# Attention in pairs of heads, and a state space branch in pairs of states, in a two-block network on one core

## The chip, the core and the metric

The kernel runs on one core of a Trainium2 chip. The metric is the device time of one execution in microseconds (us). The engines are named as in the profile: TensorE (PE, with its loads of stationary tiles as PEld), VectorE (DVE), ScalarE (ACT), GpSimd (POOL) and SyncE (SP), which here only issues DMAs.

## The reference

One sequence of 256 tokens with 1024 features goes through two blocks. The first adds a mixer with four gated branches (rwkv7, spatial gating, short convolution, state space) and a feed-forward part; the second adds an attention mixer and a feed-forward part that picks experts. What the change touches is the state space branch (16 groups of 16 channels, 64 complex states each)

```python
    bu_re = jnp.einsum('gnc,bsgc->bsgn', bb_re, ug)
    bu_im = jnp.einsum('gnc,bsgc->bsgn', bb_im, ug)
    ...
    _, _, x_re, x_im = lax.associative_scan(_complex_affine_combine, (ar, ai, bu_re, bu_im), axis=1)
    y = (jnp.einsum('gcn,bsgn->bsgc', c_re, x_re) - jnp.einsum('gcn,bsgn->bsgc', c_im, x_im))
```

and the two attentions of the second block, with 8 heads of 64 each. With 256 tokens MoBA's one block is the whole causal sequence, and forgetting attention adds a difference of cumulated log gates to the scores:

```python
    s = (jnp.einsum('bhqd,bhkd->bhqk', qi, k).astype(jnp.float32) * scale
         + cq[..., None] - c[:, :, None, :])
    ...
    s = jnp.where(kpos[None, :] <= qpos[:, None], s, -jnp.inf)
    p = jax.nn.softmax(s, axis=-1).astype(v.dtype)
    return jnp.einsum('bhqk,bhkd->bhqd', p, v)
```

## The kernel before

Activations lie transposed: features on partitions, the 256 tokens along the free axis. `linear` streams weights in units of eight 128x128 tiles (512 KB). For each unit SP loads `raw`, ScalarE rounds it to `whi` (L206), VectorE forms the rest `wlo` (L209), and POOL a part of it where `pool_k` is above 0 (L211). Each buffer exists three times. TensorE runs three matmuls for a tile (`mm3`, L231 to L233), so 24 for a unit, each with 256 tokens. These matmuls are the stream.

The smaller computations are Python generators. `spawn` enters one with a rate, and after each half of a pair of output tiles `linear` calls `tick`, which adds half the rate to its credit and runs a generator for one step per whole credit. So the rate says how many steps of a branch stand between two units of the stream. A scheduler then places the instructions of each engine.

State space: a group of 4 states is folded into 128 partitions, 8 steps `s` in all. `s5_main` (L1040) takes state `s` through: `bu` by two matmuls in a row group of 32 (L1054); products with the tables of cosines and sines (L1057, L1058, VectorE); two sums on POOL give the rotated `z`; two scans (L1064); products back (L1066, L1067); two sums on POOL give `xx` (L1069, L1070); and, two steps later, `project` with two matmuls in a column group of 32 (L1076, L1077). Rate 1.2. Beside it runs the chunked `wkv` (its matmuls L786 to L851, its masked products `kn` on POOL, L814) and the sums of `ada_all` (L426).

Attention: one function for both (L1341 on). A step handles four heads at different stages: scores of head h (L1353, in the row half of 64 that the head's features lie in, with L1355 for the gates in forgetting attention), transposes of head h - 2 (L1360), the softmax of head h - 1 on VectorE and ScalarE (L1367 to L1375), the weighted sum of head h - 3 in a column half of 64 (L1382, L1383). Rates 1.5 and 1.2. `fox_c` prepares the gates: `fw` and `frh` on VectorE (L1336, L1338) and two products into `selh` on POOL (L1337). PSUM tiles of both branches come from a ring of six, "ax".

## Time and profile before

| what | value |
|---|---|
| median of 3 runs | 1589.32 us (1588.9 to 1591.75) |
| the profiled execution, its own time | 1588.85 us |
| its span from the first to the last instruction | 1587.1 us |
| mean granted clock of TensorE | 0.987 of full speed |
| TensorE busy | 1533.5 us, 97% of the span |
| VectorE, ScalarE, POOL busy | 1134.1, 839.8, 358.7 us |
| state space branch beside wkv | from about 115 to 205 us |
| MoBA attention | from about 560 to 625 us |
| forgetting attention | from about 625 to 697 us |

The span is 1.75 us shorter than the time of the same execution. The engines' shares are means over stages with different limits, so each of the three stages is read by itself: its busy times, the waits of TensorE in it, and then single rows. A row of the timeline gives the start, the length, the engine and line, the operation, the tile written and those read, and how many pass records it stands for; neighbours of one kind are one row, and ends of matmuls are modelled, so starts are what is subtracted.

### The profile page before, as it was taken

To read this page: it belongs to the slowest core of one execution; us is meant where nothing else is said; L and a number is where in the kernel's file an instruction comes from. 1 tells how busy PE (TensorE), PEld (TensorE's weight loads), DVE (VectorE), ACT (ScalarE), POOL (GpSimd) and SP (SyncE) were. 2 spreads that over 40 slices of the span, in tenths; PEclk is the share of its full clock that TensorE was granted. 3 is DMA by queue.
4 is the path that set the end of the run, shared out by engine and by line. 5 is a ranking of instruction groups with operands and counts; after the bars stand their busy time and mean duration, and the time that the engine had idled before them with its cause. 6 is when DMAs were issued, how large, how long until landed. Compare 5 with 4: busy or idle time off the path is not lost. (4 is left out here: it accounts for less than half of the span.)

```text
span 1587.1 us, 28930 instructions
## 1 busy us (share of the span) xinstructions
PE 1533.5 (97%) x11462; PEld 1423.3 (90%) x11462; DVE 1134.1 (71%) x1800; ACT 839.8 (53%) x1399; POOL 358.7 (23%) x319
## 2 busy tenths in 40 slices
PE   6998999999999989999999999999999999999997
PEld 5887899999999978899999999999998888888886
DVE  7789886886555675667779967888898555555555
ACT  4563234756543455545445547777776445544443
POOL 7516663345400120004781700000000000000000
PEclk9899899999999999999999999999999999999999
DMA  9445456475556643445555564444544566666663
GB/s 364 153 162 159 158 192 221 152 259 189 187 184 187 189 130 108 130 135 200 173 161 192 167 187 147 146 149 144 150 152 165 174 209 186 191 194 194 193 196 121
DMA packets 75448, 279.67 MB, mean 176 GB/s; under 512 B 8368, under 2 KB 9008, under 8 KB 73648
## 3 DMA queue, kind: packets, MB, share of 16 engines
q1 hardware_dynamic: 75312, 277.82, 54.3%
q8 instruction: 90, 1.47, 0.4%
q14 instruction: 46, 0.38, 0.1%
HBM read 275.69 MB, written 2.10 MB: 175 GB/s over the span
## 5 line engine op out<-in xcount | busy, mean ns | idle before, releaser
L206 ACT ACTIVATE whi<-raw 128x1024 fp32r<-128x1024 f32 x453 | 479.1, 1058 | 551.4 <-PE mm L232 210.8
L209 DVE TENSOR_TENSOR wlo<-raw,whi 128x1024 fp32r<-128x1024 f32 (+2 forms) x413 | 500.2, 1213 | 265.3 <-ACT whi L206 262.2
L231 PE MATMUL mm<-hh,whi 128*128 128x256 f32 x1816 | 525.1, 289 | 3.1 <-ACT gate L581 1.9
L233 PE MATMUL mm<-hh,wlo 128*128 128x256 f32 x1816 | 516.1, 284 | 5.0 <-DVE wlo L209 4.2
L232 PE MATMUL mm<-hl,whi 128*128 128x256 f32 x1816 | 513.0, 282 | 1.1 <-DVE hl L1484 0.7
L231 PEld LDWEIGHTS mm<-hh,whi 128*128 128x128 f32 x1816 | 345.1, 190 | 11.4 <-issue 7.6
L233 PEld LDWEIGHTS mm<-hh,wlo 128*128 128x128 f32 x1816 | 345.8, 190 | 7.4 <-DVE wlo L209 5.0
L232 PEld LDWEIGHTS mm<-hl,whi 128*128 128x128 f32 x1816 | 346.4, 191 | 2.9 <-issue 1.4
L211 POOL TENSOR_TENSOR wlo<-raw,whi 128x256 fp32r<-128x256 f32 (+2 forms) x112 | 186.3, 1668 | 138.7 <-ACT whi L206 85.5
L1518 PE MATMUL ax<-whi,ah 128*128 128x512 f32 x512 | 158.9, 391 | 3.9 <-ACT ah L332 3.9
L1518 PE MATMUL ax<-whi,al 128*128 128x512 f32 x512 | 158.3, 391 | 0.0
L1518 PE MATMUL ax<-wlo,ah 128*128 128x512 f32 x512 | 158.1, 390 | 0.0
L1518 PEld LDWEIGHTS ax<-whi,ah 128*128 128x128 f32 x512 | 96.0, 188 | 23.8 <-ACT ah L332 4.1
L1518 PEld LDWEIGHTS ax<-whi,al 128*128 128x128 f32 x512 | 96.5, 189 | 20.5 <-DVE al L333 0.4
L1518 PEld LDWEIGHTS ax<-wlo,ah 128*128 128x128 f32 x512 | 96.4, 188 | 20.0
L1442 ACT ACTIVATE om<-xres,tg 128x128 f32<-128x128 f32 x256 | 84.9, 392 | 1.0 <-DVE xres L1439 1.0
L233 PE MATMUL ax<-hh,wlo 128*128 128x258 f32 x256 | 72.8, 284 | 1.3 <-DVE wlo L209 1.3
L231 PE MATMUL mm<-fh,whi 128*128 128x256 f32 x256 | 73.0, 285 | 0.0
L233 PE MATMUL mm<-fh,wlo 128*128 128x256 f32 x256 | 72.9, 285 | 0.0
L232 PE MATMUL mm<-fl,whi 128*128 128x256 f32 x256 | 72.9, 285 | 0.0
L231 PE MATMUL ax<-hh,whi 128*128 128x258 f32 x256 | 72.6, 284 | 0.0
L232 PE MATMUL ax<-hl,whi 128*128 128x258 f32 x256 | 72.2, 282 | 0.0
(538 smaller groups left out, 2424.1 us busy)
## 6 DMA issues: line engine op xcount, KB each, us to landing
raw<-in_wts SPq DMA_DIRECT2D x453, 512.0 KB, 3.6
raw<-in_ada SPq DMA_DIRECT2D x24, 512.0 KB, 4.2
araw<-in_ada SPq DMA_DIRECT2D x8, 1024.0 KB, 8.0
w0r<-in_w SPq DMA_DIRECT2D x8, 576.0 KB, 9.0
araw<-in_ada SPq DMA_DIRECT2D x8, 512.0 KB, 4.6
x<-in_x SPq DMA_DIRECT2D x1, 1024.0 KB, 5.1
mb<-in_x SPq DMA_DIRECT2D x2, 512.0 KB, 4.9
selh<-in_att SPq DMA_DIRECT2D x1, 1024.0 KB, 7.2
```

The costliest lines, as they stand in the source:

```text
L206: nc.scalar.activation(hi, raw, AF.Copy)
L209: nc.vector.tensor_tensor(lo[:, :c], raw[:, :c], hi[:, :c].bitcast(FT), op=OP.subtract)
L211: nc.gpsimd.tensor_tensor(lo[:, c:], raw[:, c:], hi[:, c:].bitcast(FT), op=OP.subtract)
L231: mm(ps, wh, xh, start=start, stop=False, **kw)
L232: mm(ps, wh, xl, start=False, stop=False, **kw)
L233: mm(ps, wl, xh, start=False, stop=stop, **kw)
L1442: SC.activation(om[:, j, :], oe[:, j, :], AF.Copy, scale=it["g"][:, t0 + j:t0 + j + 1])
L1518: T.matmul(acc[t][c], a[:, u, z], w[:, c * 512:(c + 1) * 512], start=i + u == 0 and n == 0, stop=i + u == P - 1 and n == 2)
```

## The change

Attention works on pairs of heads. `scores` of a pair interleaves the matmuls of the two row halves, `turn` transposes both heads, `weigh` interleaves the two column halves, and `soft` runs twice in one step. A pair has its own sequence of three steps (scores with the turn of the pair before; softmax; weighted sum), 15 steps instead of 11, and the rates go from 1.5 and 1.2 to 2.05 and 1.65. The tile of scores has four buffers instead of three.

The state space branch works on pairs of states. The bu matmuls of both states stand interleaved in two row groups of 32; the scans write in place; the products after the scan are kept as `v1`, `v2`; POOL's `xx` sums are gone. Instead `project` runs four matmuls for a state, which add the products up in PSUM: with the coefficients of plane 0, of a new plane 2 with the opposite sign, and twice of plane 1. A pair's projection stands directly behind the bu matmuls of the next pair. There are 9 steps instead of 10. In the setup one more VectorE operation fills plane 2.

```diff
@@ -446,7 +446,7 @@
             pa = es.enter_context(tc.tile_pool(name="pa", bufs=1))
             hh, hl = self.hh, self.hl
             self.s5b = pa.tile([P, 2, 2, P], FT, name="s5b")
-            self.s5c = pa.tile([P, 2, 8, 32], FT, name="s5c")
+            self.s5c = pa.tile([P, 3, 8, 32], FT, name="s5c")
             self.tab = pa.tile([P, 2, 8, S], FT, name="s5t")
             self.s5m = pa.tile([P, 8], FT, name="s5m")
             self.masks = pa.tile([P, 3, P], FT, name="masks")
@@ -1008,6 +1008,7 @@
         V.tensor_tensor(c1, craw[:, 0], b(qr), op=OP.mult)
         V.tensor_tensor(c2, craw[:, 1], b(qi), op=OP.mult)
         V.tensor_tensor(self.s5c[:, 0], c1, c2, op=OP.subtract)
+        V.tensor_tensor(self.s5c[:, 2], c2, c1, op=OP.subtract)
         V.tensor_tensor(c1, craw[:, 0], b(qi), op=OP.mult)
         V.tensor_tensor(c2, craw[:, 1], b(qr), op=OP.mult)
         V.scalar_tensor_tensor(self.s5c[:, 1], c1, -1.0, c2, op0=OP.mult, op1=OP.subtract)
@@ -1040,18 +1041,11 @@
     def s5_main(self, psum, pw, u, yo):
         nc, tc = self.nc, self.tc
         V, SC, G, T = nc.vector, nc.scalar, nc.gpsimd, nc.tensor
-        todo, yps = [], {}
-        for s in range(8):
...
+        yps = {}
+
+        def states(s, bu):
             cb = self.tab[:, 0, s:s + 1, :].to_broadcast([P, 2, S])
             sb = self.tab[:, 1, s:s + 1, :].to_broadcast([P, 2, S])
-            bu = psum.tile([P, 2, S], FT, name="ax")
-            for i in range(2):
-                T.matmul(bu[:, i, :], self.s5b[R, h, i, :], u[R, h, :], start=True, stop=True)
             t1, t2 = pw.tile([P, 2, S], FT, name="t1"), pw.tile([P, 2, S], FT, name="t2")
             z = pw.tile([P, 2, S], FT, name="z")
             V.tensor_tensor(t1, bu, cb, op=OP.mult)
@@ -1059,31 +1053,44 @@
             G.tensor_tensor(z[:, 0, :], t1[:, 0, :], t2[:, 1, :], op=OP.add)
             G.tensor_tensor(z[:, 1, :], t1[:, 1, :], t2[:, 0, :], op=OP.subtract)
             m = self.s5m[:, s:s + 1].to_broadcast([P, S])
-            sc = pw.tile([P, 2, S], FT, name="sc")
+            sc = z
             for i in range(2):
                 V.tensor_tensor_scan(sc[:, i, :], m, z[:, i, :], 0.0, op0=OP.mult, op1=OP.add)
-            t1, t2 = pw.tile([P, 2, S], FT, name="t1"), pw.tile([P, 2, S], FT, name="t2")
-            V.tensor_tensor(t1, sc, cb, op=OP.mult)
...
+            v1, v2 = (pw.tile([P, 2, S], FT, name=n, bufs=2) for n in ("v1", "v2"))
+            V.tensor_tensor(v1, sc, cb, op=OP.mult)
+            V.tensor_tensor(v2, sc, sb, op=OP.mult)
+            return v1, v2
+
+        def project(p, vs):
+            h, q = divmod(2 * p, 4)
+            if q == 0:
+                yps[h] = psum.tile([P, S], FT, name="ax")
+            yp = yps[h]
+            for t, (c, j, i) in enumerate(((0, 0, 0), (2, 1, 1), (1, 0, 1), (1, 1, 0))):
+                for a in range(2):
+                    R = slice(32 * (q + a), 32 * (q + a) + 32)
+                    T.matmul(yp[R, :], self.s5c[:, c, 2 * p + a, :], vs[a][j][:, i, :], start=t == 0, stop=t == 3)
+            if q == 2:
+                y = pw.tile([P, S], FT, name="y5", bufs=1)
+                V.scalar_tensor_tensor(y, u[:, h, :], self.v("s5_d", h), yp, op0=OP.mult, op1=OP.add)
+                SC.activation(yo[:, h, :], y, AF.Gelu_apprx_tanh)
+
+        vs = {}
+        for p in range(4):
+            h, q = divmod(2 * p, 4)
             yield
-            project()
+            bus = [psum.tile([P, 2, S], FT, name="ax") for _ in range(2)]
+            for i in range(2):
+                for a in range(2):
+                    R = slice(32 * (q + a), 32 * (q + a) + 32)
+                    T.matmul(bus[a][:, i, :], self.s5b[R, h, i, :], u[R, h, :], start=True, stop=True)
+            if p:
+                project(p - 1, vs)
+            vs[0] = states(2 * p, bus[0])
+            yield
+            vs[1] = states(2 * p + 1, bus[1])
+        yield
+        project(3, vs)
 
     def conv(self, zp, bg, y):
         V = self.nc.vector
@@ -1277,10 +1284,10 @@
             self.selh = selh
             self.linear(psum, hh, hl, 12, 8, evac, outer=True)
             self.linear(psum, hh, hl, 1, 8, lambda n, ps: evac(n + 12, ps), groups=[1])
-            self.spawn(self.attention(psum, pd, qa, ka, vt["a"], amask, None, oh[:, 0], ol[:, 0]), 1.5)
+            self.spawn(self.attention(psum, pd, qa, ka, vt["a"], amask, None, oh[:, 0], ol[:, 0]), 2.05)
             self.linear(psum, hh, hl, 12, 8, lambda n, ps: evac(n + 13, ps))
             self.drain()
-            self.spawn(self.attention(psum, pd, qb, kb, vt["b"], amask, self.fox, oh[:, 1], ol[:, 1]), 1.2)
+            self.spawn(self.attention(psum, pd, qb, kb, vt["b"], amask, self.fox, oh[:, 1], ol[:, 1]), 1.65)
             self.linear(psum, hh, hl, 16, 8, lambda n, ps: evac(n + 25, ps))
             merged = t("mg", [P, 8, S])
             mh, ml = t("mh", [P, 8, S], FR), t("ml", [P, 8, S], FR)
@@ -1342,48 +1349,62 @@
         nc = self.nc
         V, SC, G, T = nc.vector, nc.scalar, nc.gpsimd, nc.tensor
         parts = ((0, 128), (128, 256))
-        sp, s, pp, op = {}, {}, {}, {}
-        for step in range(8 + 3):
...
+        half = [slice(0, 64), slice(64, 128)]
+        sp, s, pt = {}, {}, {}
+
+        def scores(c):
+            for a in range(2):
+                sp[a] = psum.tile([P, 384], FT, name="ax")
+            for i, (o, n) in enumerate(parts):
+                for a, R in enumerate(half):
+                    T.matmul(sp[a][:, o:o + n], q[R, c, i * P:(i + 1) * P], k[R, c, 0:n], start=True, stop=fox is None)
+                if fox:
+                    for a in range(2):
+                        F = slice(64 * a, 64 * a + 40)
+                        T.matmul(sp[a][:, o:o + n], fox[0][F, 2 * c + a, i * P:(i + 1) * P], fox[1][F, 0:n],
+                                 start=False, stop=True)
+
+        def soft(a):
+            s[a] = pd.tile([P, 384], FT, name="sc", bufs=4)
+            V.scalar_tensor_tensor(s[a], sp[a], -0.125, amask, op0=OP.mult, op1=OP.add)
+            mx = pd.tile([P, 4], FT, name="mx", bufs=3)
+            for i, (o, n) in enumerate(parts):
+                V.tensor_reduce(mx[:, i:i + 1], s[a][:, o:o + n], axis=AX.X, op=OP.min)
+                SC.activation(s[a][:, o:o + n], s[a][:, o:o + n], AF.Exp, bias=mx[:, i:i + 1], scale=-1.0,
+                              accum_out=mx[:, 2 + i:3 + i])
+            V.reciprocal(mx[:, 2:4], mx[:, 2:4])
+            for i, (o, n) in enumerate(parts):
+                V.tensor_scalar(s[a][:, o:o + n], s[a][:, o:o + n], mx[:, 2 + i:3 + i], None, op0=OP.mult)
+
+        def turn():
+            for a in range(2):
+                pp = psum.tile([P, 384], FT, name="ax")
                 for b in range(3):
-                    T.transpose(pp[h][:, b * P:(b + 1) * P], s[h][:, b * P:(b + 1) * P], self.ident)
-                pt = pd.tile([P, 384], FT, name="pt", bufs=3)
...
+                    T.transpose(pp[:, b * P:(b + 1) * P], s[a][:, b * P:(b + 1) * P], self.ident)
+                pt[a] = pd.tile([P, 384], FT, name="pt", bufs=3)
+                SC.activation(pt[a], pp, AF.Copy)
+
+        def weigh(c):
+            op = psum.tile([P, S], FT, name="ax")
+            for i, (z, o) in enumerate(((slice(0, S), slice(0, S)), (slice(128, S), slice(256, 384)))):
+                for a, R in enumerate(half):
+                    h = 2 * c + a
+                    T.matmul(op[R, z], vt[:, i, h * 64:(h + 1) * 64], pt[a][:, o], start=i == 0, stop=i == 1)
+            SC.activation(oh[:, c, :], op, AF.Copy)
+            V.tensor_tensor(ol[:, c, :], op, oh[:, c, :].bitcast(FT), op=OP.subtract)
+
+        for c in range(4 + 1):
+            if c < 4:
+                scores(c)
+            if c:
+                turn()
+            yield
+            if c < 4:
+                soft(0)
+                soft(1)
+            yield
+            if c:
+                weigh(c - 1)
             yield
 
     def peer(self):
```

On TensorE, where state 0 is projected: before, its two matmuls (`xx`) ahead of the bu of state 2, with the stream behind.

```order
L799 MATMUL ax_1663<-main_63,kt_1331 128x128 x2
L1076 MATMUL ax_1670<-xx_1476,s5c_80 32x256
L1077 MATMUL ax_1670<-xx_1476,s5c_80 32x256
L1054 MATMUL ax_1673<-uD_86,s5b_79 128x256 x2
L231 MATMUL mm_1624<-hh_70,whi_1549 128x256
L232 MATMUL mm_1624<-hl_71,whi_1549 128x256
```


After, in the same place, four matmuls of bu for states 2 and 3 (tiles ax_1663 and ax_1664), and then the projection of states 0 and 1; four more matmuls on `v1` and `v2` follow.

```order
L799 MATMUL ax_1656<-main_63,kt_1332 128x128 x2
L1086 MATMUL ax_1663<-uD_86,s5b_79 128x256
L1086 MATMUL ax_1664<-uD_86,s5b_79 128x256
L1086 MATMUL ax_1663<-uD_86,s5b_79 128x256
L1086 MATMUL ax_1664<-uD_86,s5b_79 128x256
L1072 MATMUL ax_1669<-v1_1475,s5c_80 32x256
L1072 MATMUL ax_1669<-v1_1589,s5c_80 32x256
L1072 MATMUL ax_1669<-v2_1476,s5c_80 32x256
L1072 MATMUL ax_1669<-v2_1590,s5c_80 32x256
```


The projection went behind bu, doubled its matmuls, and now takes in state 1's products. On TensorE again, a step of forgetting attention in its middle, before: scores of one head, transposes of another, the weighted sum of a third.

```order
L1353 MATMUL ax_7592<-kb_6180,qb_6179 128x128
L1355 MATMUL ax_7592<-frh_6667,selh_6174 128x128
L1353 MATMUL ax_7592<-kb_6180,qb_6179 128x256
L1355 MATMUL ax_7592<-frh_6667,selh_6174 128x256
L1360 MATMUL ax_7597<-main_63,sc_7516 128x128 x3
L1382 MATMUL ax_7526<-pt_7514,vtb_6182 64x256
L1383 MATMUL ax_7526<-pt_7514,vtb_6182 64x128
```


After, the scores of a pair and the transposes of the pair before; the weighted sum (L1392) stands by itself, one and a half to three units of the stream later.

```order
L1360 MATMUL ax_7416<-kb_6165,qb_6164 128x128
L1360 MATMUL ax_7417<-kb_6165,qb_6164 128x128
L1364 MATMUL ax_7416<-frh_6652,selh_6159 128x128
L1364 MATMUL ax_7417<-frh_6652,selh_6159 128x128
L1360 MATMUL ax_7416<-kb_6165,qb_6164 128x256
L1360 MATMUL ax_7417<-kb_6165,qb_6164 128x256
L1364 MATMUL ax_7416<-frh_6652,selh_6159 128x256
L1364 MATMUL ax_7417<-frh_6652,selh_6159 128x256
L1383 MATMUL ax_7426<-main_63,sc_7333 128x128 x3
L1383 MATMUL ax_7432<-main_63,sc_7343 128x128 x3
```


Two heads' scores became one block. On VectorE at the start of MoBA attention, before: the gates (`fw`, `frh`), then the softmax of heads 0 (`sc_6775`) and 1 (`sc_6825`), with a weight split between.

```order
L1336 TENSOR_SCALAR fw_6668<-fu_6658 8x256
L1338 TENSOR_SCALAR frh_6667<-fu_6658 8x256
L1367 SCALAR_TENSOR_TENSOR sc_6775<-ax_6738,atc_6172 128x384
L1370 TENSOR_REDUCE mx_6777<-sc_6775 128x1 x2
L1367 SCALAR_TENSOR_TENSOR sc_6825<-ax_6772,atc_6172 128x384
L209 TENSOR_TENSOR wlo_6788<-raw_6785,whi_6787 128x1024
L1373 RECIPROCAL mx_6777<-mx_6777 128x2
L1370 TENSOR_REDUCE mx_6827<-sc_6825 128x1
L1375 TENSOR_SCALAR sc_6775<-sc_6775,mx_6777 128x128
L1375 TENSOR_SCALAR sc_6775<-sc_6775,mx_6777 128x256
```


After (head 0 is `sc_6729`, head 1 `sc_6739`; the masking of head 0 stands ahead of the gates):

```order
L1343 TENSOR_SCALAR fw_6653<-fu_6643 8x256
L1345 TENSOR_SCALAR frh_6652<-fu_6643 8x256
L1278 TENSOR_TENSOR qb_6164<-mm_6661,r2_6161 128x512
L1375 RECIPROCAL mx_6731<-mx_6731 128x2
L1369 SCALAR_TENSOR_TENSOR sc_6739<-ax_6693,atc_6157 128x384
L1377 TENSOR_SCALAR sc_6729<-sc_6729,mx_6731 128x128
L1377 TENSOR_SCALAR sc_6729<-sc_6729,mx_6731 128x256
L1372 TENSOR_REDUCE mx_6741<-sc_6739 128x1 x2
L209 TENSOR_TENSOR wlo_6753<-raw_6750,whi_6752 128x1024
L1375 RECIPROCAL mx_6741<-mx_6741 128x2
L1377 TENSOR_SCALAR sc_6739<-sc_6739,mx_6741 128x128
L1377 TENSOR_SCALAR sc_6739<-sc_6739,mx_6741 128x256
```


Head 0's scale (L1377) moved ahead of the weight split, head 1's stands behind it, and a scaling of forgetting attention's queries (`qb`) stands between the gates and both.

## Rows read from the trace of the kernel before

**Rows 1.** the page's first section: busy us, share of span, instructions by engine.

```profile
PE 1533.5 (97%) x11462; PEld 1423.3 (90%) x11462; DVE 1134.1 (71%) x1800; ACT 839.8 (53%) x1399; POOL 358.7 (23%) x319
```

**Rows 2.** busy time by stretch: stretch, length, engines, granted clock, DMA share, GB/s.

```profile
115.00:205.00 90.00, 81.41 (x810) 70.42 (x808) 80.50 (x103) 26.20 (x37) 56.16 (x53) 0.94 0.51 166
158.20:161.40 3.20, 3.20 (x16) 3.20 (x16) 2.30 (x3) 0.57 (x1) 3.20 (x5) 0.50 0.89 349
560.00:625.00 65.00, 59.19 (x428) 51.88 (x427) 43.47 (x80) 35.20 (x72) 9.21 (x2) 0.95 0.36 114
578.00:584.60 6.60, 3.38 (x16) 3.30 (x17) 6.60 (x14) 2.67 (x8) 1.63 (x1) 0.50 0.27 79
625.00:697.00 72.00, 72.00 (x528) 63.88 (x527) 43.10 (x79) 35.24 (x70) 0.00 (x0) 1.00 0.39 122
```

**Rows 3.** TensorE's waits at L831: waiter, releaser, us in all, times, longest.

```profile
PE ax L831 <- POOL kn L814: 2.5, 1, 2.5
PE ax L831 <- POOL xx L1069: 1.2, 1, 1.2
```

**Rows 4.** timeline of TensorE in both attentions: start, length, instruction, passes.

```profile
570.04 0.29 PE L233 MATMUL mm<-hh,wlo 128*128 128x256 f32 x1
570.40 0.28 PE L233 MATMUL mm<-hh,wlo 128*128 128x256 f32 x1
...
571.68 0.28 PE L232 MATMUL mm<-hl,whi 128*128 128x256 f32 x1
...
646.23 0.28 PE L233 MATMUL mm<-hh,wlo 128*128 128x256 f32 x1
...
647.94 0.55 PE L1360 MATMUL ax<-main,sc 128*128 128x128 f32 x3
648.41 0.65 PE L1382 MATMUL ax<-pt,vtb 128*64 128x256 f32 x2
...
649.43 0.28 PE L232 MATMUL mm<-hl,whi 128*128 128x256 f32 x1
```

**Rows 5.** the same view: groups of matmuls that use parts of the array.

```profile
22.47 1.07 PE L509 MATMUL ap<-araw,cap 128*32 128x256 f32 x16
...
104.65 1.09 PE L1130 MATMUL ax<-sgw,t 128*64 128x128 f32 x16
...
122.10 1.14 PE L786 MATMUL ax<-ar,bt 64*128 64x256 f32 x8
```

**Rows 6.** the same view: state 0's bu alone, then project(0) and state 2's bu.

```profile
126.97 0.28 PE L233 MATMUL mm<-hh,wlo 128*128 128x256 f32 x1
...
128.45 0.28 PE L232 MATMUL mm<-yl,whi 128*128 128x256 f32 x1
...
136.22 0.62 PE L1076 MATMUL ax<-xx,s5c 128*32 128x256 f32 x2
...
137.20 1.12 PE L1054 MATMUL ax<-uD,s5b 32*128 32x256 f32 x4
138.26 0.39 PE L231 MATMUL mm<-hh,whi 128*128 128x256 f32 x1
```

**Rows 7.** timeline of all engines around MoBA's first transposes.

```profile
570.12 4.68 POOL L1337 TENSOR_TENSOR selh<-selh,fw 8x2048 f32<-8x2048 f32 x1 [19.90 <-DVE fw L1336]
...
570.37 4.58 DVE L1336 TENSOR_SCALAR fw<-fu 8x256 f32<-8x256 f32 x1
...
575.10 4.53 POOL L1337 TENSOR_TENSOR selh<-selh,fw 8x2048 f32<-8x2048 f32 x1 [0.30 <-DVE fw L1336]
...
576.89 3.82 DVE L209 TENSOR_TENSOR wlo<-raw,whi 128x1024 fp32r<-128x1024 f32 x1
...
581.22 0.95 PE L1360 MATMUL ax<-main,sc 128*128 128x128 f32 x3 [5.81 <-DVE sc L1375]
```

**Rows 8.** timeline of VectorE: state 1's last product.

```profile
140.27 0.68 DVE L1067 TENSOR_TENSOR t<-sc,s5t 128x512 f32<-128x512 f32 x1
```

**Rows 9.** one line's instructions: count, shortest/median/longest ns, first and last start.

```profile
L1010 DVE TENSOR_TENSOR s5c<-c,c x1: 959/959/959, 32.0 to 32.0; 128x256 f32<-128x256 f32 x1
```

More of the change, by code (lines that the diff above doesn't have):

```diff
@@ L1042, in s5_main @@
         V, SC, G, T = nc.vector, nc.scalar, nc.gpsimd, nc.tensor
-        todo, yps = [], {}
-        for s in range(8):
-            h, q = divmod(s, 4)
-            yield
-            if len(todo) == 2:
-                todo.pop(0)()
-            R = slice(32 * q, 32 * q + 32)
+        yps = {}
+        def states(s, bu):
             cb = self.tab[:, 0, s:s + 1, :].to_broadcast([P, 2, S])
             sb = self.tab[:, 1, s:s + 1, :].to_broadcast([P, 2, S])
-            bu = psum.tile([P, 2, S], FT, name="ax")
-            for i in range(2):
-                T.matmul(bu[:, i, :], self.s5b[R, h, i, :], u[R, h, :], start=True, stop=True)
             t1, t2 = pw.tile([P, 2, S], FT, name="t1"), pw.tile([P, 2, S], FT, name="t2")
@@ L1061, in s5_main @@
             m = self.s5m[:, s:s + 1].to_broadcast([P, S])
-            sc = pw.tile([P, 2, S], FT, name="sc")
+            sc = z
             for i in range(2):
                 V.tensor_tensor_scan(sc[:, i, :], m, z[:, i, :], 0.0, op0=OP.mult, op1=OP.add)
-            t1, t2 = pw.tile([P, 2, S], FT, name="t1"), pw.tile([P, 2, S], FT, name="t2")
-            V.tensor_tensor(t1, sc, cb, op=OP.mult)
-            V.tensor_tensor(t2, sc, sb, op=OP.mult)
-            xx = pw.tile([P, 2, S], FT, name="xx", bufs=2)
@@ L1069, in s5_main @@
-            G.tensor_tensor(xx[:, 0, :], t1[:, 0, :], t2[:, 1, :], op=OP.subtract)
-            G.tensor_tensor(xx[:, 1, :], t1[:, 1, :], t2[:, 0, :], op=OP.add)
-            def project(R=R, s=s, h=h, q=q, xx=xx):
-                if q == 0:
-                    yps[h] = psum.tile([P, S], FT, name="ax")
-                yp = yps[h]
-                T.matmul(yp[R, :], self.s5c[:, 0, s, :], xx[:, 0, :], start=True, stop=False)
-                T.matmul(yp[R, :], self.s5c[:, 1, s, :], xx[:, 1, :], start=False, stop=True)
-                if q == 3:
-                    y = pw.tile([P, S], FT, name="y5", bufs=1)
-                    V.scalar_tensor_tensor(y, u[:, h, :], self.v("s5_d", h), yp, op0=OP.mult, op1=OP.add)
-                    SC.activation(yo[:, h, :], y, AF.Gelu_apprx_tanh)
@@ L1083, in s5_main @@
-            todo.append(project)
-        for project in todo:
-            yield
-            project()
+            v1, v2 = (pw.tile([P, 2, S], FT, name=n, bufs=2) for n in ("v1", "v2"))
[15 more added lines that the diff above has]
+                SC.activation(yo[:, h, :], y, AF.Gelu_apprx_tanh)
```

37 lines of the change are left out of this document (removed).

## Prediction

> **What bounds the kernel now.** I read the page's first section, then the busy time by stretch of the three places that the change touches, then TensorE's waits, and last single rows. TensorE is busy for 97% of the span [rows 1], so what the change is worth is what it takes off TensorE's instruction stream, less any new idle time there. The stretches differ. In 625 to 697 us (forgetting attention beside its stream of weight tiles) TensorE is busy for 72.00 of 72 us while VectorE has 43.10 and ScalarE 35.24: only TensorE's own work counts. In 560 to 625 (MoBA attention) it has 59.19 of 65, with a hole and a stretch at granted clock 0.50 (that is 1.2 of 2.4 GHz) behind it. In 115 to 205 (state space branch beside the chunked wkv) it has 81.41 of 90, but VectorE has 80.50: there a wait on VectorE is as likely as a gain on TensorE [rows 2]. Of that stretch's waits two belong here: matmul L831 stood 2.5 us for POOL's kn and 1.2 us for POOL's xx [rows 3].
>
> How I price work put into the stream: matmuls of the stream start every 0.12 us (three in 570.04 to 570.40), so an insertion costs the start of the second stream matmul behind it, less that of the last one ahead, less 0.24. An f32 matmul is two passes, and a row's count is one of passes.
>
> **Forgetting attention, one head before.** From 646.23 to 649.43: 3.20 less 0.24 is 2.96 us, of which the scores (8 passes) take 1.59, three transposes 0.47 (647.94 to 648.41) and the weighted sum (4 passes) the other 0.90 [rows 4]. Whether a pair costs as much as a head depends on two halves of the array running at once. Rows of before that do it: L786, two row halves of 64, has 8 passes of 256 columns in 1.14 us; L1130, two column halves, 16 passes of 128 columns in 1.09; L509, four column groups, 16 passes of 256 columns in 1.07 [rows 5]. Against these stand L1054, one 32-row group, with 4 such passes in 1.12, and L1076 with L1077, one column group, 4 passes in 0.98 (136.22 to 137.20) [rows 6]. So two halves cost one, and I price a pair's scores and sums like a head's: 1.59 + 2 x 0.47 + 0.90 = 3.43.
>
> Each place where the stream is opened also has an entry: L1054 alone costs 1.24 (126.97 to 128.45, less 0.24), and directly behind other work 1.06 (137.20 to 138.26), so 0.18 [rows 6]. By the order the eight heads stood at 11 places and the four pairs stand at 9. Before: 8 x 2.96 + 3 x 0.18 = 24.2. After: 4 x 3.43 + 5 x 0.18 = 14.6. **Gain 9.6.** Nothing waits in this stretch now, and with 62 us left VectorE's 43.10 is still 70% of it, so I charge no new wait. If that cover is gone, it is rival D. Loads of the stationary tiles run on the other queue beside the matmuls (63.88 of 72 us [rows 2]); their number per matmul is unchanged here.
>
> **MoBA attention.** Its scores are four passes: 1.04 alone (570.40 to 571.68 [rows 4]), 0.9 within a block; a head is 0.9 + 0.47 + 0.90 = 2.3, a pair 0.9 + 0.94 + 0.90 = 2.74. By the order, 10 places before and 8 after: 8 x 2.3 + 2 x 0.18 = 18.8 against 4 x 2.74 + 4 x 0.18 = 11.7. Gain 7.1. Less the hole: TensorE stood 5.81 us, until 581.22, for the normalized scores of head 0 (L1375). VectorE was late because fw (L1336) took 4.58 us beside one POOL product into selh (from 570.12) and a weight split 3.82 us beside the next (575.10 to 579.63) [rows 7]. The new order lets TensorE come earlier: the first scores 24 matmuls (2.9 us) sooner, then 72 matmuls (8.6) and the second pair's scores (1.0); counted from 566.6, where the first scores stood (570.5, behind the matmul of 570.40, less 24 matmuls and 1.04), it is at the transposes at 574.4 instead of 575.4 (581.22 less 5.81). VectorE's queue there is fw, frh, a qb product, then head 0's normalization, the weight split, and head 1's. Head 1's scale stands behind the split: if the scale of head 0 too is held up by the product into selh, as fw was, TensorE goes on at 582.0 (the product's end at 579.63, and an estimate of 2.4 for two scales, reductions and a split); if only the split is held up, at 580.7 (581.22 as now, less 0.47, since head 0's transposes are done by then). The stall is 6.3 to 7.6. I take 7.6, nearest to fw, which is the same kind of instruction (tensor_scalar): 1.8 more than now. **Gain 5.3** (6.6 by the other end).
>
> On that choice the Trainium skill (SBUF — State Buffer, section "SBUF: two separate sides") has a rule: VectorE and GpSimd share a port pair that is locked for a whole instruction by a VectorE op in a fast mode or with two SBUF inputs, or by a GpSimd op, and the loser is blocked. By that rule both the scale and the split wait, which is 582.0 and the sum as forecast, and without it the time would be 1.3 less; the trace agrees for fw (4.58) and the split (3.82).
>
> **State space branch.** Before, on TensorE: two states' bu alone, six with the projection of an earlier state (0.98 + 1.06 = 2.04), two projections alone: 2 x 1.24 + 6 x 2.04 + 2 x (0.98 + 0.18) = 17.0 [rows 6]. After, a pair's bu is 8 passes in two 32-row groups, and its projection 16 passes in two 32-column groups. No row shows two 32-row groups at once; bounds are 1.06 (as L786 overlaps its 64-row halves) and twice 4 passes, 1.94; I take 1.06, since that row is the nearest. The projection is 8 slots of 0.245: 1.96. Sum: 1.24 + 3 x (1.06 + 1.96) + 1.96 + 0.18 = 12.4. Gain 4.6 (1.1 by the other bound).
>
> A new wait goes against it. project(0) now stands directly behind the second bu pair, one step after state 1, and needs state 1's products. With the bu pair ahead, TensorE would be there at 137.3 (136.22 + 1.06), while state 1's last product ended before at 140.27 + 0.68 = 140.95 [rows 8]. A wait of 3.5 is new there, about; queued behind it on TensorE is the whole stream, and with it VectorE's evacuation. The later pairs I take as served, since POOL loses 16 operations. Bounds: 0, if that relief brings VectorE forward by as much, and twice 3.5, if a second pair is late too or the clock falls: behind the 2.5 wait at 156 us came 3.20 us at clock 0.50 with 16 matmuls, which costs 1.6 [rows 2]. The wait for xx (1.2) goes with xx. The wait for kn (2.5) stays: POOL's z of state 3 still stands ahead of it. **Gain 4.6 - 3.5 + 1.2 = 2.3.** VectorE's own count per state is unchanged; the sign that POOL gave is in a third plane of coefficients, one more VectorE op of the kind of L1010, 0.96 us [rows 9], at 32 us, between 0 (hidden) and 0.96: **loss 0.5**.
>
> **Sum.** 9.6 + 5.3 + 2.3 - 0.5 = 16.7 off the profiled 1588.85: 1572.15. The median, 1589.32, is 0.47 above it, so 1572.6.
>
> **Rivals.**
> A, the state space gain is eaten by waits: with VectorE busy for 80.50 of 90 us, every pair's second state comes late. Its 2.3 becomes between -4 and 0: 1574.9 to 1578.9. For it: VectorE's load, and the measured late products. Against: POOL's two sums between a state's products and its projection are out of that chain.
> B, the relief pays in full: no wait at project(0), the wait for xx gone, 4.6 + 1.2 = 5.8 instead of 2.3, and the hole in MoBA as now (+1.8): 1567.3. For it: POOL is busy for 56.16 of 90. Against: state 1's products were late by 3.5 through VectorE, not POOL, in row order.
> C, slower: halves run one behind the other. Then the second half costs again: 4 x (1.41 + 0.72) = 8.5 in forgetting attention, 4 x 1.44 = 5.8 in MoBA, 4 x 0.88 + 4 x 1.96 = 11.4 in the branch, 25.7 in all, and the change costs 9.0: 1598.3. It turns slower once 65% of the overlap is missing. The projection is where it would be felt first, since its matmuls are doubled. The halves that run at once, in both directions of the array [rows 5], speak against it.
> D, evacuation: TensorE is ready, scores of a pair are not. Eight turns, each 1 to 1.5 us late: 8 to 12 less gain, 1580.6 to 1584.6. For it: VectorE must treat two heads in one go, and six tiles of PSUM serve pairs. Against: 70% load.
> The Trainium skill (TensorEngine Tiling (Array Packing), "PSUM Bottleneck") says that packing speeds TensorE and not the evacuation of PSUM, which may then bound. That rule gives D's time; the 43.10 of 72 us does not bear it out in this stage.
>
> **How the numbers follow.** Forecast case 62% (1568 to 1575), A 17%, B 10%, C 4%, D 7%. The range takes in B and A and most of D's near end: 1564 to 1582, leaving out about 10% of these cases and as much for what I have not seen. A run of this kernel tells some 0.2%, 3.2 us, from no change: slower has C, and a tail of A and D together, 6%; same 5%; faster 89%.
>
> **What would show it.** Right: TensorE busy throughout the forgetting stage, and that stage some 9.6 us shorter; L786-like rows of 8 passes in about 1.1 us for the score pairs and the bu pairs; one wait of 6 to 8 us at the first transposes; one of about 3.5 at project(0). Wrong: a row of 8 passes in 2 us, TensorE waits for VectorE at each turn, granted clock 0.50 where it was 1.00.

## The result

The changed kernel takes 1573.79 us (median of 4 runs, 1572.57 to 1577.32); the kernel before, run beside it, 1590.53. The ratio is 0.9898 with a 95% interval from 0.9882 to 0.9913: about 16 us faster, where 16.7 were forecast, and 1573.79 where 1572.6 was.

The two profiles can be laid side by side exactly, since both run the same 8016 stream matmuls. The table gives the time between the starts of the same stream matmul in both (the stretch borders are matmuls number 0, 528, 1400, 3456, 3840 and 4300, counted from the first L231). The first scores of forgetting attention stand ahead of number 3840 in both, so they count to MoBA's stretch.

| stretch (before, us) | what lies there | before | after | gain | forecast |
|---|---|---|---|---|---|
| 18 to 109 | setup, plane 2 of s5c | 90.17 | 90.17 | 0.0 | -0.5 |
| 109 to 294 | state space branch, wkv, ada_all | 185.91 | 185.20 | 0.7 | 2.3 |
| 294 to 555 | untouched | 260.19 | 260.87 | -0.7 | 0 |
| 555 to 628 | MoBA attention | 73.60 | 67.61 | 6.0 | 5.3 |
| 628 to 705 | forgetting attention | 76.99 | 66.39 | 10.6 | 9.6 |

With 0.3 lost ahead of the first matmul the rows add up to the difference of the spans, 1587.1 and 1570.8. So the total came out nearly as forecast, from two attentions that gave 1.7 more than forecast and a branch that gave 1.6 less.

### The profile page after: what moved, and what is told of

Read it like the earlier page. It is cut to its first block, busy times and chain, and to the rows that moved or that the text cites. A ratio compares the mean times of both kernels' runs of the same rounds, so it can differ in the third digit from the quotient of the medians.

```text
span 1570.8 us, 28981 instructions
## 1 busy us (share of the span) xinstructions
PE 1515.3 (96%) x11494; PEld 1412.3 (90%) x11494; DVE 1132.9 (72%) x1801; ACT 837.0 (53%) x1399; POOL 345.7 (22%) x303
## 4 chain that ended last, share of the span: by engine, by line
PE 46%; DVE 2%; POOL 1%; issue 1%; ACT 0%; DVEq 0%; ACTq 0%
PE ax L1539 22%; PE mm L233 7%; PE mm L232 7%; PE mm L231 7%; PE ax L1470 4%; POOL wlo L211 1%; POOL GT L1604 0%; DVE GT L1636 0%; DVE wlo L209 0%; DVE GT L1634 0%; PE ax L1577 0%; DVE GT L1553 0%; ACT whi L206 0%; DVE GT L1614 0%; DVE GT L1615 0%
## 5 line engine op out<-in xcount | busy, mean ns | idle before, releaser
L231 PE MATMUL mm<-hh,whi 128*128 128x256 f32 x1816 | 524.8, 289 | 3.7 <-ACT gate L581 2.5
L231 PEld LDWEIGHTS mm<-hh,whi 128*128 128x128 f32 x1816 | 344.9, 190 | 10.3 <-issue 5.2
L1539 PEld LDWEIGHTS ax<-whi,ah 128*128 128x128 f32 x512 | 96.0, 188 | 23.9 <-ACT ah L332 4.1
L231 PE MATMUL mm<-fh,whi 128*128 128x256 f32 x256 | 73.0, 285 | 0.0
L231 PE MATMUL ax<-hh,whi 128*128 128x258 f32 x256 | 72.6, 284 | 0.0
```

Of the source, the lines that this page charges most:

```text
L231: mm(ps, wh, xh, start=start, stop=False, **kw)
L1539: T.matmul(acc[t][c], a[:, u, z], w[:, c * 512:(c + 1) * 512], start=i + u == 0 and n == 0, stop=i + u == P - 1 and n == 2)
```

## The profile after

The first section of the page, as [rows 1]:

```profile
PE 1515.3 (96%) x11494; PEld 1412.3 (90%) x11494; DVE 1132.9 (72%) x1801; ACT 837.0 (53%) x1399; POOL 345.7 (22%) x303
```

The busy times by stretch, as [rows 2] (stretch, length, engines, granted clock, DMA share, GB/s); the three half-clock rows are those behind waits:

```profile
115.00:205.00 90.00, 79.19 (x845) 68.29 (x846) 84.89 (x108) 27.72 (x40) 49.87 (x43) 0.93 0.52 167
141.90:145.30 3.40, 3.40 (x15) 1.80 (x12) 3.40 (x6) 0.00 (x0) 0.66 (x1) 0.50 0.51 142
203.30:206.70 3.40, 3.40 (x17) 1.29 (x16) 3.40 (x3) 1.12 (x3) 3.40 (x3) 0.50 0.51 149
561.10:622.60 61.50, 55.89 (x452) 51.17 (x450) 45.22 (x81) 35.71 (x74) 9.22 (x2) 0.94 0.43 127
578.80:585.60 6.80, 5.35 (x24) 4.88 (x25) 6.76 (x14) 4.35 (x11) 0.00 (x0) 0.50 0.47 137
622.60:689.00 66.40, 66.40 (x567) 63.09 (x566) 45.18 (x83) 35.10 (x71) 0.00 (x0) 1.00 0.48 145
```

Forgetting attention is still bound by TensorE, 66.40 of 66.40, though VectorE is at 68% and ScalarE at 53%. In the branch TensorE is busy for less, 79.19 against 81.41, in the same 90 us. TensorE's waits show why (waiter, releaser, us in all, times, longest), as [rows 3]:

```profile
PE ax L1383 <- DVE sc L1377: 5.6, 2, 4.2
PE ax L831 <- DVE s L852: 3.9, 2, 3.2
...
PE ax L1072 <- DVE v L1060: 2.0, 1, 2.0
...
PE ax L831 <- POOL kn L814: 1.4, 1, 1.4
```

The timeline of TensorE in forgetting attention, as the second half of [rows 4], with the scores of a pair and the transposes of the one before:

```profile
631.12 0.28 PE L233 MATMUL mm<-hh,wlo 128*128 128x256 f32 x1
631.33 0.49 PE L1360 MATMUL ax<-kb,qb 64*128 64x128 f32 x4
631.65 0.39 PE L1364 MATMUL ax<-frh,selh 40*128 40x128 f32 x4
631.88 0.60 PE L1360 MATMUL ax<-kb,qb 64*128 64x256 f32 x4
632.31 0.60 PE L1364 MATMUL ax<-frh,selh 40*128 40x256 f32 x4
632.84 0.88 PE L1383 MATMUL ax<-main,sc 128*128 128x128 f32 x6
633.47 0.36 PE L231 MATMUL mm<-hh,whi 128*128 128x256 f32 x1
```

From 631.12 to 632.84, less 0.12, the 16 passes of a pair's scores take 1.60; the 8 passes of one head took 1.59 [rows 4]. The second head costs nothing. The six transposes take 0.63 (632.84 to 633.47).

## The experiments

All were run with the kernel before beside them. A ratio is that to the kernel before. Stretches are those of the table above, each read from one profile. Two kernels, one half and in turn (e3 and e4), ran once each (1580.19 and 1572.05 us), so only their stretches and rows are used.

**Attention alone, and the branch alone.** Each undoes one part of the change. The first (e1) has the whole old `s5_main` again, two coefficient planes, and the old setup; the second (e2) the whole old `attention` and its rates. Of the first, and then of the second:

```diff
-            self.s5c = pa.tile([P, 3, 8, 32], FT, name="s5c")
+            self.s5c = pa.tile([P, 2, 8, 32], FT, name="s5c")
...
-        V.tensor_tensor(self.s5c[:, 2], c2, c1, op=OP.subtract)
...
```

```diff
-            self.spawn(self.attention(psum, pd, qa, ka, vt["a"], amask, None, oh[:, 0], ol[:, 0]), 2.05)
+            self.spawn(self.attention(psum, pd, qa, ka, vt["a"], amask, None, oh[:, 0], ol[:, 0]), 1.5)
...
-            self.spawn(self.attention(psum, pd, qb, kb, vt["b"], amask, self.fox, oh[:, 1], ol[:, 1]), 1.65)
+            self.spawn(self.attention(psum, pd, qb, kb, vt["b"], amask, self.fox, oh[:, 1], ol[:, 1]), 1.2)
...
```

> The kernel before with the change in the two attentions alone. By my theory (nearly all of the gain is theirs) the stretch of MoBA attention gets shorter by about 6.0 us and that of forgetting attention by about 10.6, as between the two profiles, and the whole by 16 to 17: ratio 0.989 to 0.990, the state space stretch as before. Rival (the forecast's own split, 14.9 for attention and 2.3 for the state space branch): 2 us less gain than the whole change, ratio near 0.9905, which only the stretches can tell apart.

> The kernel before with the change in the state space branch alone. Theory: TensorE's own work there falls by about 3.8 us (bu and projection 16.4 to 12.6), and longer waits (about 2) and half-clock stretches (about 1.4) give nearly all of it back: the same time within 1 us, ratio 0.9995 to 1.0005. Rival (the forecast): 1.8 us faster with the extra setup operation in it. Second rival: the gain comes only with the attention change, then the time is unlike both.

Attention alone: 1576.05 us, ratio 0.9907 (0.9890 to 0.9925). MoBA 67.74 and forgetting attention 66.39, as with the whole change (67.61 and 66.39). The branch alone: 1591.46 us, ratio 1.0001 (0.9989 to 1.0012). So the attentions carry the gain and the pairs of states alone give none that can be measured; the forecast's 1.8 is 0.9989, the very end of the interval. By the whole time of attention alone, its rival (0.9905) would fit as well as its theory (0.989 to 0.990); the stretches decide. Its state space stretch took 187.50, where the kernel before took 185.91 with the same instructions.

**One half of the array for both heads.** To see whether the overlap of halves, and not the fewer openings of the stream, is what pays, both heads of a pair use the same row half (so the second head's scores are left out of what this kernel computes):

```diff
-                for a, R in enumerate(half):
+                for a, R in enumerate((half[0], half[0])):
...
-                        F = slice(64 * a, 64 * a + 40)
+                        F = slice(0, 40)
```

> The changed kernel, but the scores of both heads of a pair are computed in the same row half of 64, so head 1 gets head 0's scores (that part of the computation is changed); all else is as it was. Theory (two halves of the array run at once): the second head's passes come behind the first's, 8 passes in one row of L1360 where they took 0.93 us take about 1.8, a pair's scores cost 0.86 more in MoBA and 1.4 more in forgetting attention, the stretch of the latter gets 5.5 to 6 us longer (66.4 to 72), that of MoBA 2.5 to 3.5. Rival (the gain came from fewer openings of the stream, not from halves at once): both stretches change by under 1 us.

The timeline of TensorE at the same block of this kernel:

```profile
635.17 0.28 PE L233 MATMUL mm<-hh,wlo 128*128 128x256 f32 x1
635.38 0.71 PE L1360 MATMUL ax<-kb,qb 64*128 64x128 f32 x4
...
636.38 1.03 PE L1360 MATMUL ax<-kb,qb 64*128 64x256 f32 x4
...
638.20 0.88 PE L1383 MATMUL ax<-main,sc 128*128 128x128 f32 x6
```

The scores of the pair take 2.91 (635.17 to 638.20, less 0.12) instead of 1.60. The stretch of forgetting attention went from 66.39 to 70.31: its border cuts off the first pair, and three times 1.31 is 3.9. The expected 1.4 a pair is right within 0.1; the 5.5 to 6 in the expectation had counted four pairs. MoBA's stretch, which holds that first pair, became 2.0 longer (69.61): four times 0.65 (0.86 expected) and once 1.31 are 3.9, but its wait was 1.3 shorter and half clock cost 0.7 less. The rival, under 1 us, is out.

**One head's matmuls ahead of the other's.** The same exchange of loops was made in `weigh`.

```diff
-            for i, (o, n) in enumerate(parts):
-                for a, R in enumerate(half):
+            for a, R in enumerate(half):
+                for i, (o, n) in enumerate(parts):
```

> The changed kernel, but in scores and weighted sums the matmuls of one head all stand ahead of those of the other, in different halves as before. Theory (TensorE starts its matmuls in their order and runs two halves at once only where neighbours use different halves): most of the overlap goes, 1.1 to 1.4 us per pair of scores in forgetting attention and 0.5 to 0.65 per weighted sum, so that stretch goes from 66.4 to 72 to 74 us. Rival (the halves have queues of their own, order does not matter): the stretch stays at 66.4 within 0.5.

The theory that the order makes the overlap fell for the most part. MoBA's scores and the weighted sums take what they took interleaved; only the scores of forgetting attention, with eight matmuls instead of four, lose 0.54 a pair (2.14 against 1.60, from 628.21 to 630.47, less 0.12), and their stretch is 68.06 instead of 66.39. The timeline of TensorE, MoBA's scores and then a weighted sum of forgetting attention, in the changed kernel:

```profile
573.71 0.93 PE L1360 MATMUL ax<-ka,qa 64*128 64x128 f32 x8
...
642.19 0.87 PE L1392 MATMUL ax<-pt,vtb 128*64 128x256 f32 x8
```

and with the heads in turn, with the borders of a pair's scores of forgetting attention between:

```profile
589.66 0.93 PE L1360 MATMUL ax<-ka,qa 64*128 64x128 f32 x8
...
628.21 0.28 PE L233 MATMUL mm<-hh,wlo 128*128 128x256 f32 x1
...
630.47 0.87 PE L1382 MATMUL ax<-main,sc 128*128 128x128 f32 x6
...
639.82 0.88 PE L1391 MATMUL ax<-pt,vtb 128*64 128x256 f32 x8
```

Eight passes in 0.93 and in 0.88, as interleaved. So TensorE ran two halves at once although two whole matmuls of one head stood ahead of the other's.

**Gates by copies instead of POOL's products.** This takes away what I held to delay VectorE at MoBA's first transposes.

```diff
-            nc.gpsimd.tensor_tensor(lh[b:b + 8], lh[b:b + 8], c[:, None, :].to_broadcast([8, 8, S]), op=OP.mult)
+            for h in range(8):
+                nc.sync.dma_start(lh[b + h:b + h + 1, h, :], w[b + h:b + h + 1, :])
```

> The changed kernel, with POOL's two products into selh replaced by sixteen 1 KB copies on the SP queue (one row of gates for each head onto the diagonal of selh; its other elements stay zero). Theory: VectorE's fw (4.6 us) and the scale of head 0 (3.5 us for two) were held up by these POOL products. With them gone fw takes 0.3, the scale 0.5, the two waits at the first transposes (4.16 and 1.45) go, and with them most of the 6.8 us at half clock: 6 to 9 us faster than the changed kernel, ratio to the kernel before about 0.985. Rival: the wait is the softmax's own length (masking, reductions, exponentials, scale); then fw still gets short, but the waits stay above 3 us and the time moves by less than 2. Slower if the sixteen copies delay weight loads on SP: TensorE would wait for wlo in 565 to 580.

First the changed kernel's timeline of all engines there, as [rows 7]:

```profile
574.13 4.53 POOL L1344 TENSOR_TENSOR selh<-selh,fw 8x2048 f32<-8x2048 f32 x1 [0.30 <-DVE fw L1343]
...
575.02 0.54 DVE L1369 SCALAR_TENSOR_TENSOR sc<-ax,atc 128x384 f32<-128x384 f32 x1
575.47 3.54 DVE L1377 TENSOR_SCALAR sc<-sc,mx 128x128 f32<-128x128 f32 x2
...
578.80 0.95 PE L1383 MATMUL ax<-main,sc 128*128 128x128 f32 x3 [4.16 <-DVE sc L1377]
...
581.20 0.87 PE L1383 MATMUL ax<-main,sc 128*128 128x128 f32 x3 [1.45 <-DVE sc L1377]
```

The two scales of head 0 take 3.54 us beside POOL's product. The first of them, 3.28 of these, lasts until POOL's product ends (574.13 + 4.53 = 578.66); the masking with one input in PSUM, beside the same product, takes its usual 0.54. And with the copies:

```profile
568.25 8.19 SPq L1345 DMA_DIRECT2D selh<-fw  x13
...
568.55 0.28 DVE L1343 TENSOR_SCALAR fw<-fu 8x256 f32<-8x256 f32 x1
...
570.32 0.54 DVE L1378 TENSOR_SCALAR sc<-sc,mx 128x128 f32<-128x128 f32 x2
...
573.72 0.88 PE L1384 MATMUL ax<-main,sc 128*128 128x128 f32 x6
```

```profile
554.10:613.50 59.40, 59.40 (x504) 55.22 (x502) 40.24 (x83) 39.10 (x79) 0.00 (x0) 1.00 0.47 149
```

The second fw takes 0.28, the scales 0.54, TensorE has no idle time in MoBA and no half clock (the last row is its busy time by stretch). The stretch falls from 67.61 to 59.34, the kernel to 1564.81 us, ratio 0.984 (0.982 to 0.986): 9 us under the changed kernel. The amount fits as well: the changed kernel's 67.61 less its idle time (5.61) and less what half clock added (2.67) is 59.33. So it is shown that POOL's products held up VectorE, and that this caused the wait and the half clock behind it. By its median this is the fastest version of the study.

**The branch.** What gives back the branch's saved work? First, the projection one step later, so that it does not wait for state 1:

```diff
+            return sc, cb, sb
+
+        def back(sc, cb, sb):
             v1, v2 = (pw.tile([P, 2, S], FT, name=n, bufs=2) for n in ("v1", "v2"))
...
             if p:
+                vs[1] = back(*st)
+            st = states(2 * p, bus[0])
+            yield
+            if p:
                 project(p - 1, vs)
-            vs[0] = states(2 * p, bus[0])
-            yield
-            vs[1] = states(2 * p + 1, bus[1])
+            vs[0] = back(*st)
+            st = states(2 * p + 1, bus[1])
+        yield
+        vs[1] = back(*st)
         yield
         project(3, vs)
```

> The changed kernel with the projection of a pair one step later, and each state's last two products moved into the step of the next state. Theory: the wait at project(0) (2.03 us, and half clock behind it) goes, since the products of state 1 are ready; but the wait of L831 at the end, 3.19 us on VectorE's updates L852 behind the last state's operations, is another matter and stays or moves by under 1 us. 2 to 4 us faster than the changed kernel in the stretch 110 to 225 us. Rival: the stretch is bound by VectorE as a whole, and a wait that is taken away at one place comes back at the next L831 or L847: same time within 1 us.

1575.83 us, ratio 0.9905 (0.9888 to 0.9922); the stretch to 294 us 187.5. The waits at the projection and of L831 on L852 are gone, and others have come:

```profile
PE ax L847 <- ACT bt L837: 4.7, 2, 3.2
...
PE ax L831 <- DVE s L834: 1.4, 1, 1.4
```

The rival was right that the wait comes back at the next L847; the stretch was even 2.3 longer than the changed kernel's 185.2. Its reason, VectorE as a whole, is not shown by this: the new wait is for ScalarE. On top of the copies I then ran the old branch (e7: attention alone, with the copies), and the pairs with more of the weight split on POOL (e9), at two other rates (e10, e11) and with slower sums of ada_all (e12); e13 is e7 with those slower sums. The edits of e9, e10 and e12 (e11 has 1.5 for 0.9):

```diff
-            self.pool_k = 2
+            self.pool_k = 3
```

```diff
-            self.spawn(self.s5_main(psum, p5, uD, yf[:, 3]), 1.2, "s5")
+            self.spawn(self.s5_main(psum, p5, uD, yf[:, 3]), 0.9, "s5")
```

```diff
-            self.spawn(self.ada_all(psum, pe_), 1.7)
+            self.spawn(self.ada_all(psum, pe_), 1.0)
```

> The kernel before with the attention change and the copies in place of POOL's products, and with its own state space branch. Theory (the branch in pairs gives nothing of its own): the time of the changed kernel with the copies within 1.5 us, 1564 to 1567. Rival (the forecast: pairs of states are worth 1.8): 1566 to 1567 and a stretch 110 to 226 us longer by 2.

> The changed kernel with the copies, and with three eighths of each weight split on POOL instead of two in the stretch of the state space branch (21 units: VectorE's part 128x640 instead of 128x768). Theory (that stretch is bound by VectorE, 98 of 106 us busy, and the waits of TensorE there are VectorE's lateness): VectorE gives up about 21 x 0.15 = 3 us, the waits of L831 and L1072 get 1 to 3 us shorter, and the time falls by 1 to 4 us. Rival (POOL's work holds VectorE up when both work from SBUF, or L831's wait for POOL's kn grows from 3.3): same time or up to 4 us slower.

> The changed kernel with the copies in place of POOL's products, and the state space branch at rate 0.9 instead of 1.2, so that its states lie further apart among the updates of wkv. Theory (TensorE's 3.2 us wait at L831 came because the operations of the last state stood ahead of the updates L852 in VectorE's order, and VectorE had no room between): with the states apart that wait and half clock behind it go, the stretch from 109 to 226 us gets 2 to 5 us shorter than with the copies alone (116.3), unless the branch's end moves behind 226; whole 1560 to 1564. Rival (VectorE's work in the stretch is what counts, wherever it stands): the waits move to other L831 or L1072, the stretch within 1.5 us.

> As the one with the copies, but the state space branch at rate 1.5. Theory: the states lie closer together on VectorE, so the first projections wait longer (1.7 us now) and the updates L834 and L852 come later: the stretch gets 1 to 4 us longer. Rival (VectorE's work counts wherever it stands): the stretch within 1.5 us of 116.3.

> The changed kernel with the copies, and the sums of ada_all (L426 on VectorE, 1.3 to 1.9 us each) at rate 1.0 instead of 1.7: some seven of the fourteen between 109 and 226 us move behind, where VectorE is busy for 46 of 69 us. Theory (the saved TensorE work of the pairs of states is given back because VectorE has no room in that stretch): VectorE gets some 9 us there, TensorE's waits at L1072 and L831 (together 8 us and the half clock behind them) get at least 3 us shorter, and the stretch to 294 us falls from 184.6 to 178 to 181. Rival (the waits are chains of dependent steps, not VectorE's load): 183 us or more.

> The same slower ada_all, with the copies and the attention in pairs, but the state space branch of the kernel before. Theory: with room on VectorE TensorE's own work decides, so the pairs of states are worth 2 to 4 us between this and the kernel with pairs: the stretch from 109 to 294 us is longer here by that. Rival (pairs give nothing even then): equal within 1 us.

The border between the two columns of stretches is stream matmul number 1008.

| kernel | median, us | ratio (interval) | 109 to 226, us | 226 to 294, us |
|---|---|---|---|---|
| e5, pairs with the copies | 1564.81 | 0.9840 (0.9820 to 0.9860) | 116.26 | 68.38 |
| e7, old branch with the copies | 1567.72 | 0.9846 (0.9822 to 0.9870) | 117.57 | 69.84 |
| e9, three eighths on POOL | 1572.54 | 0.9880 (0.9858 to 0.9902) | 119.29 | 71.80 |
| e10, branch at 0.9 | 1567.31 | 0.9849 (0.9817 to 0.9880) | 113.70 | 76.78 |
| e11, branch at 1.5 | 1567.32 | 0.9852 (0.9820 to 0.9884) | 117.03 | 69.78 |
| e12, ada_all at 1.0 | 1580.44 | 0.9947 (0.9924 to 0.9969) | 116.74 | 68.76 |
| e13, old branch, ada_all at 1.0 | 1577.87 | 0.9915 (0.9892 to 0.9937) | 118.01 | 69.78 |

The old branch with the copies (e7) is 2.9 us behind the pairs by the medians, with intervals that overlap, and 2.6 us of that lie ahead of 109 us in its profile, where both run the same instructions but for the one that fills plane 2. That decides neither its theory nor its rival. At rate 0.9 the wait on L852 at L831 goes and the first column falls by 2.6, as the theory had it, but the branch ends behind 226 us (its last projection at 245) and the second column gives back 8.4. That is the exception that the expectation named, not its rival. At 1.5 the stretch keeps its length, which is the rival's bound too; a projection waits 3.5 us there instead. Slower sums of ada_all test the load on VectorE itself. Its busy time in the stretch (109 to 225 with the copies, 109 to 225.6 with slower sums):

```profile
109.00:225.00 116.00, 103.11 (x1160) 90.88 (x1159) 104.45 (x138) 34.46 (x50) 58.24 (x49) 0.96 0.54 169
```

```profile
109.00:225.60 116.60, 102.40 (x1145) 91.01 (x1144) 94.38 (x129) 34.82 (x49) 52.53 (x49) 0.93 0.45 139
```

VectorE had 10 us less to do, and the stretch did not get shorter (116.74 against 116.26). TensorE's longest wait there even grew, to the first of these two:

```profile
PE ax L831 <- DVE s L834: 5.0, 1, 5.0
...
PE ax L831 <- DVE s L852: 3.2, 2, 2.0
```

So by this pair of profiles it is not VectorE's load as such, and the theory that I had for e12 fell: the waits at L1072 and L831 came to 8.2 us in all where they had been 9.2 with the copies, and 3 less were expected. The lengths alone would say less, since half clock cost 3.7 us more between 109 and 294 us than with the copies (10.3 against 6.6). (e12 and e13 lose 12 to 14 us between 294 and 555, where ada_all then ends; I did not follow that up.) Between e12 and e13 the pairs are 2.3 us ahead in the stretch to 294 us and 2.6 behind by the medians: nothing is decided there. That leaves the chains of wkv and of the states, each a dozen steps over three engines, and their places relative to each other. That they decide is argued, not shown, and which of their steps set the end is open. More of the split on POOL made it worse by 3 us in each column, the opposite of its theory, which speaks for POOL's and VectorE's work holding each other up, but this one kernel does not show the cause.

How much the pairs of states are worth is hard to see for a reason of its own. Five profiles run the same instructions up to 294 us with pairs (the changed kernel, e2 to e5), three with single states (the kernel before, e1, e7). Their TensorE time from 109 to 294 us, split into the branch's own matmuls, idle gaps, what half clock added, and the rest:

| profiles | branch's matmuls | gaps | half clock | the stretch, mean | from, to |
|---|---|---|---|---|---|
| three with single states | 16.4 | 12.1 | 7.3 | 186.9 | 185.9, 187.5 |
| five with pairs | 12.6 | 13.9 | 8.8 | 186.2 | 184.6, 187.9 |

The pairs save about 3.8 us of TensorE's work in every profile. Gaps grow by 1.8 and half clock by 1.5, and 0.7 is left, less than the 3.2 by which profiles of the same instructions differ. The most exact measure of the pairs by themselves is the branch alone: its interval (0.9989 to 1.0012) goes from 1.8 us faster to 1.9 us slower.

## Why the prediction was right

**Forgetting attention, 9.6 forecast, 10.6 measured.** The step that two halves cost one is shown by the pair (1.60 against 1.59) and by e3. The term that was mis-sized is the transposes: I had priced three at 0.47 and six at 0.94, and six take 0.63. By the starts in both timelines, all openings of the stream together cost 23.9 before (priced 24.2) and 13.3 after (priced 14.6), and most of the difference is in the transposes. No wait took the place of the gain: rival D, evacuation, did not come at 68% of VectorE. The Trainium skill says that packing does not speed the evacuation of PSUM, which may then bound (TensorEngine Tiling (Array Packing), "PSUM Bottleneck"); this stage has not reached that limit. Rival C, halves one behind the other, did not come; e3 shows its price for these scores, 1.31 a pair where 1.41 was taken.

**MoBA, 5.3 forecast, 6.0 measured.** TensorE's own work fell by 6.7 us (the stretch without idle time and without what half clock added went from 66.0 to 59.3), forecast 7.1. TensorE was at the transposes at 574.64 (578.80 less 4.16), forecast 574.4, and waited 5.61 in two parts, where 7.6 were forecast and 5.81 was before. The choice of the blocked scale was right: 3.54 us for two scales that take 0.54 with the copies, the first held until POOL's product ends. The Trainium skill (SBUF — State Buffer, "SBUF: two separate sides") names VectorE operations in a two-port mode or with two SBUF inputs as those that share a lock with GpSimd. The scale has a single SBUF tensor; that it ran in such a mode, no view here shows. The size was off by 2.0, because the gates' products ran 1 us earlier (574.13 instead of 575.10 [rows 7]), where I had left them as they were, and because head 0's transposes, 0.95 at half clock, lie inside the wait; TensorE also came 0.2 later. Against that, half clock behind it cost 2.7 instead of 1.8, a term that the sum did not have.

**The branch, 2.3 forecast, 0.7 measured, and not to be told from 0.** Here a step failed, and the outcome lies nearer to rival A's upper end, 0, than to the forecast. TensorE's own work fell by 3.8 where 4.6 was priced, and two 32-row groups run at once, which no row of before had shown:

```profile
137.36 1.13 PE L1086 MATMUL ax<-uD,s5b 32*128 32x256 f32 x8
138.42 0.62 PE L1072 MATMUL ax<-v,s5c 128*32 128x256 f32 x2
141.08 0.41 PE L1072 MATMUL ax<-v,s5c 128*32 128x256 f32 x2 [2.03 <-DVE v L1060]
```

This is the timeline of TensorE at project(0): eight passes of bu in 1.13 where four took 1.12 [rows 6], and then the new wait, 2.03 instead of 3.5, with half clock from 141.9 on. What failed is "The wait for xx (1.2) goes with xx", booked as a gain. The wait for POOL went, but TensorE's waits at L831 grew in all from 3.9 us (2.5 for kn, 1.2 for xx, 0.2 for L852) to 5.7 (1.4 for kn, 0.4 for another product of L814, 3.9 for L852): a wait for VectorE came at the same line. The timelines of VectorE and of TensorE at the last L831:

```profile
199.87 1.03 DVE L1060 TENSOR_TENSOR v<-z,s5t 128x512 f32<-128x512 f32 x1
200.83 0.68 DVE L1061 TENSOR_TENSOR v<-z,s5t 128x512 f32<-128x512 f32 x1
201.43 0.41 DVE L852 TENSOR_TENSOR s<-s,ax 128x256 f32<-128x256 f32 x1
```

```profile
201.89 0.68 PE L831 MATMUL ax<-s,kn 64*64 64x64 f32 x16 [3.19 <-DVE s L852]
```

State 7's scan and products stand ahead of the update L852, TensorE waits 3.19 us for that update, and half clock follows (203.3 to 206.7). The prediction asked what is late next at project(0), and not at this place. Its other error was to take [rows 2] and [rows 8] as constants of the kernel: half clock comes and goes at other places in profiles of the same instructions, and it cost 8.3 us in this stretch after and 6.8 before, which the sum held only as a bound.

**The setup, 0.5 loss forecast, none seen** (90.17 in both). This one pair of profiles does not show that the extra operation is hidden: five profiles with it took 86.43 to 91.61 us up to there, three without it 90.17 to 92.92, so a loss of 0.5 could not be seen.

That the total came within 1.2 us is in part luck: attention gave 1.7 more and the branch 1.6 less, two errors that cancel. The mechanism of the larger part, two halves at the price of one, was right.

## What to carry to other kernels

Where small matmuls leave half of TensorE's array idle, price a pair of them like one and look for what else lies in the block; here the score pairs paid in full because the stage was bound by TensorE alone. Where TensorE waits on chains over several engines, saved matmuls may buy nothing that can be measured, as in the branch: ask at every wait that goes which operation is next behind it, in the order of the engine that is waited for. And before a difference of 2 us in a stretch is explained, look how much two profiles of the same instructions differ there.

## What the runs showed of the hardware

- The order of the two halves' matmuls mattered little: with two matmuls of one half ahead of two of the other, eight passes still took 0.93 us; with four ahead of four, 16 passes took 2.14 instead of 1.60 interleaved and 2.91 in a single half.
- Two tensor_scalar operations on VectorE, 128x128 and 128x256 from SBUF to SBUF, took 3.54 us beside a POOL product of two SBUF operands, and 0.54 without it; a masking with its input in PSUM took 0.54 beside it.
- Sixteen copies of 1 KB on SP's queue, thirteen of them issued over 8.19 us, cost TensorE no wait in that stretch.
- Five profiles of the same instructions differed by 3.2 us in 185, with half-clock stretches of 3.4 or 6.8 us at different places: 18 of 24 stood at or behind a wait of TensorE of 1.4 to 3.7 us, the other six, from 254 us on, had none above 0.7 us in the 45 us ahead of them.
